# Two transformer layers with a routed mixture of experts: router weights folded with the modulation, and the last two tiles' residual sums and some of their norm statistics moved to TensorE and ScalarE

## The chip, the core and the metric

The kernel runs on one core of a Trainium2 chip. The metric is the device time of one execution, in microseconds. Beside the timed executions one more was profiled, and every row of a trace below is from that one.

## What is computed

Two layers. In each, 256 latent tokens (and in layer 0 also 256 context tokens) of width 1024 go through a token mixer, a residual sum with a layer norm, a modulated second layer norm, a router that picks 2 of 16 experts for a token, and the experts:

```python
p = modulate(h, mod[0], mod[1]) @ w_in + b_in
y = token_mix_out(p, ...)                       # ends in merged @ w_out + b_out
h = affine_ln(ALPHA * h + mod[2] * y, ln1_g, ln1_b)
m = hier_moe(modulate(h, mod[3], mod[4]), ...)  # modulate(x, shift, scale) = layer_norm(x) * (1 + scale) + shift
h = affine_ln(ALPHA * h + mod[5] * m, ln2_g, ln2_b)
...
glog, elog = tok @ rg_w + rg_b, tok @ re_w + re_b    # hier_moe: 4 groups, 16 experts
gsel = argmax(glog); top_v, top_i = top_k(elog of that group, 2)
out = sum over the chosen experts of weight * (silu(tok @ w_gate) * (tok @ w_up)) @ w_down
```

`mod` is six vectors of 1024 from one matrix product with the conditioning vector, a set for latent and a set for context tokens. Layer 1 needs latent tokens alone.

## The kernel before

Tokens are worked on in tiles of 128: in layer 0 tiles 2 and 3 are context and 0 and 1 latent, in layer 1 there are tiles 0 and 1. A tile keeps its tokens on the 128 partitions, its 1024 channels along the free axis.

Weights come in 512 KB pieces on SyncE's DMA queue, which issues in the order of the program and waits whenever the buffer of the next piece isn't free. Weights that need nearly full precision are split by ScalarE (`wh`) and VectorE (`wl`, or POOL) into two parts and multiplied in three matmuls of the fp32r type. Transposes (`tr`, L260) and other plain fp32 products (`mm`, L257) are TensorE matmuls; a plain fp32 matmul stands in the trace as two records.

The part of a layer around the change is `mix_out`. `merge` ends just before it; `mix_out` splits `merged` into `xh` and `xl`, then runs `wout` for the context tiles (layer 0 alone) and for the latent tiles, whose products ScalarE scales into `yT`, channels on partitions. `norms(tt)` transposes `yT` back in four 128 x 128 blocks for each half of a tile, VectorE adds `ALPHA * h` out of PSUM (L1206), `norm_affine` (L444 to L448) takes the first norm's statistics (`a0bst`, `a1bst`, `a0brs`, ...), and writes `h`; a second `norm_affine` with the modulation rows writes `xm` (statistics `b0...`, `b1...`), and POOL's queue sends `xm` to DRAM (`h2s`), from where the experts gather their tokens. `logits(tt)` (L1213 on) transposes `xm`, ScalarE copies it to `h2Tt`, and eight 20-column matmuls per tile with the router weights `rw` make `plog`. `route` (L1238) adds the bias `rb` into `lg` (L1242) and picks groups and experts; `rank` counts tokens of each expert and ends in `mxi` (L1311). Then every engine loads `mxi` and branches on it (L1603, L1604), and the experts start.

After the last `wout` there is no more weight work in layer 1 until the branch: what runs is this tail of norms, logits and route. In layer 0 the tail also has half of layer 1's modulation in it: `pump` hands out groups `psg<-w,silc` on TensorE over 16 pieces of `w_mod`, whose result (bank 2) goes to `mt`, `mods` in DRAM, and in part transposed into `modT` (L388 to L412). The order of the instructions on an engine is that of a scheduler at build time, so it interleaves the parts.

In layer 0 the latent tiles' `h` is loaded on POOL's queue and the position table added to it on POOL (L453 to L456) well before; POOL also does the `wl` splits of the latent `wout`.

## Time and profile before

| what | value |
|---|---|
| time of 3 runs | 1872.6, 1880.85, 1885.78 us (median 1880.85) |
| the profiled execution's own time | 1872.98 us |
| its span, first to last instruction | 1871.2 us |
| granted TensorE clock, mean | 0.958 of full speed |
| TensorE busy | 1716.1 us, 92% of the span |
| VectorE, ScalarE, POOL busy | 64%, 45%, 12% |
| DMA | 396.50 MB, 212 GB/s over the span |

The engines are PE (TensorE matmuls), PEld (its weight loads), DVE (VectorE), ACT (ScalarE), POOL (GpSimd) and SP (SyncE, DMA issue). Names as `psmm<-ident,yT` are the tile written and the tiles read, without buffer numbers. A line such as L257 can be that of a helper. A row of a timeline gives the start, the duration, the engine, the line, the operation, its operands and their shapes, how many instructions follow each other, and in square brackets how long the engine stood idle before and what ended that.

### The profile page before, as it was taken

What the parts mean: (1) busy time and instruction counts of PE and PEld (TensorE: products, weight loads), DVE (VectorE), ACT (ScalarE), POOL (GpSimd) and SP (SyncE); (2) the same over time, 40 slices, a digit from 0 to 9 for tenths busy, and PEclk for the clock granted to TensorE, in tenths of its full rate; (3) what the DMA queues carried; (4) which work ended last, traced back from release to release, by engine and by line L of the source; (5) the groups of instructions that cost most, each with busy time, mean ns of one, the idle gap of its engine ahead of it and who ended that gap; (6) DMA issues with size and microseconds to landing.
All of it is one profiled execution on the core that took longest, in us unless ns stands there. A gap on an engine that the chain in (4) does not pass through costs nothing. (4 is left out here: it accounts for less than half of the span.)

```text
span 1871.2 us, 31716 instructions
## 1 busy us (share of the span) xinstructions
PE 1716.1 (92%) x11399; PEld 1268.0 (68%) x11399; DVE 1204.7 (64%) x2623; ACT 851.3 (45%) x1696; POOL 223.1 (12%) x321
## 2 busy tenths in 40 slices
...
GB/s 342 90 75 46 13 24 152 197 84 130 169 130 192 300 144 188 304 295 398 392 382 376 345 314 77 66 92 58 47 147 149 169 327 168 324 414 406 403 410 136
DMA packets 112732, 396.50 MB, mean 212 GB/s; under 512 B 16256, under 2 KB 16352, under 8 KB 112560
## 3 DMA queue, kind: packets, MB, share of 16 engines
...
## 5 line engine op out<-in xcount | busy, mean ns | idle before, releaser
L266 ACT ACTIVATE wh<-w 128x512 fp32r<-128x512 f32 x500 | 310.1, 630 | 416.8 <-PE psmm L257 293.0
L263 DVE TENSOR_TENSOR wl<-w,wh 128x512 fp32r<-128x512 f32 x484 | 333.3, 700 | 188.6 <-ACT wh L266 185.2
L257 PE MATMUL psmm<-xh,wh 128*128 128x256 f32 (+1 forms) x1280 | 440.1, 344 | 1.3 <-ACT wh L266 1.3
L257 PE MATMUL psmm<-xh,wl 128*128 128x256 f32 (+1 forms) x1280 | 434.8, 340 | 4.0 <-POOL wl L263 2.9
L257 PE MATMUL psmm<-xl,wh 128*128 128x256 f32 (+1 forms) x1280 | 433.1, 339 | 2.0 <-DVE xl L263 2.0
L257 PEld LDWEIGHTS psmm<-xh,wh 128*128 128x128 f32 x1280 | 243.1, 190 | 52.5 <-issue 16.0
L257 PEld LDWEIGHTS psmm<-xh,wl 128*128 128x128 f32 x1280 | 243.0, 190 | 38.7 <-issue 5.9
L257 PEld LDWEIGHTS psmm<-xl,wh 128*128 128x128 f32 x1280 | 243.3, 190 | 30.0 <-issue 3.9
L970 DVE SCALAR_TENSOR_TENSOR cx<-cbuf,part,cx 128x512 f32<-128x512 f32 (+1 forms) x240 | 143.0, 614 | 2.1
L257 PE MATMUL psmm<-br,wh 128*128 128x512 f32 (+1 forms) x512 | 127.9, 337 | 0.4 <-ACT cth L266 0.4
L263 DVE TENSOR_TENSOR hid<-hid,psmm 128x256 f32<-128x256 f32 (+1 forms) x32 | 17.2, 537 | 136.6 <-PE psmm L257 121.6
L257 PEld LDWEIGHTS psmm<-br,wh 128*128 128x128 f32 x512 | 87.6, 188 | 11.7 <-ACT cth L266 0.6
L263 DVE TENSOR_TENSOR xh<-w,xh 128x512 fp32r<-128x512 f32 x124 | 80.5, 686 | 18.9 <-ACT xh L266 17.9
L257 PE MATMUL psmm<-br,wl 128*128 128x512 f32 (+1 forms) x256 | 86.4, 338 | 1.1 <-DVE wl L263 1.1
L257 PE MATMUL psmm<-xh,xTh 128*128 128x512 f32 x224 | 79.4, 413 | 5.7 <-ACT xh L266 5.1
L266 ACT ACTIVATE xh<-w 128x512 fp32r<-128x512 f32 x124 | 72.2, 627 | 18.9 <-DMA w<-in_expert_w_gate_dram 7.2
L257 PE MATMUL psg<-w,silc 128*32 128x512 f32 x320 | 64.2, 651 | 16.3 <-DMA w<-in_wmod_dram 16.3
L257 PE MATMUL psmm<-w,xTh 128*64 128x256 f32 x560 | 67.6, 387 | 1.6 <-DMA w<-in_expert_w_up_dram 1.1
L266 ACT ACTIVATE ye<-psmm,m 128x512 f32<-128x512 f32 x46 | 30.3, 684 | 71.5 <-PE psmm L257 71.1
L257 PEld LDWEIGHTS psmm<-w,xTh 128*64 128x64 f32 x560 | 41.0, 139 | 26.6 <-issue 5.1
L257 PEld LDWEIGHTS psmm<-xh,xTh 128*128 128x128 f32 x224 | 40.9, 189 | 24.5 <-ACT xh L266 9.7
L266 ACT ACTIVATE xTh<-psg 128x512 fp32r<-128x512 f32 (+1 forms) x46 | 26.3, 598 | 65.4 <-PE psg L260 62.0
...
## 6 DMA issues: line engine op xcount, KB each, us to landing
...
```

Of the source, the lines that this page charges most:

```text
L257: self.nc.tensor.matmul(out, lhsT, rhs, start=start, stop=stop, **k)
L263: (eng or self.nc.vector).tensor_tensor(out, a, b, op)
L266: self.nc.scalar.activation(out, in_, func, **k)
L970: nc.vector.scalar_tensor_tensor(x, w, dw[:, c, k:k + 1], x, op0=ALU.mult, op1=ALU.add)
```

## The change

1. `router_fold` (new): for each of latent and context tokens the router weights are multiplied by (1 + scale) of the modulation, each column's mean over the channels is taken off (a matmul with ones gives the column sums), and shift times the weights plus the bias goes into a constant `rwc`. A logit is then (weights of that kind times `h`), times the reciprocal deviation of the second norm, plus `rwc`: one small VectorE operation per tile writes `lg`. So `logits` transposes `h`, the first norm's result, and needs of the second norm the deviation `rs` alone; `modulate` still writes `xm` for `h2s`. `mod_rows` now transposes bank 2 of the modulation as well (four transposes, two copies more a layer) and leaves the 1 to be added at another place.
2. `norms_last` (new): for tiles 0 and 1, h + y / ALPHA is summed in PSUM by TensorE: for each half of a tile four fp32 matmuls of 128 columns (`yT` times identity) and one of 512 columns (identity times `h`). The first norm's epsilon is divided by ALPHA squared to match. Tile 0's first statistics are read by VectorE from PSUM. Tile 1's first statistics and both tiles' second ones are taken by ScalarE (`norm_sums`: a copy that also accumulates the sum, then a square with the mean as bias that accumulates the squares). Tiles 2 and 3 keep `norms`, with a plain addition at L1206's place.
3. The 256-column constant `pre` is dropped; its one user, inside the branch for more than 128 tokens of an expert, makes it anew.

```diff
@@ -396,17 +397,15 @@
                 nc.sync.dma_start(self.mods[l][:, o:o + 512], rows[64 * hf + 32 * m:64 * hf + 32 * m + 2, :])
-        if b == 2:
-            return
         pt = self.ps()
...
         for hf in hfs:
-            for m in ((0, 1), (0,))[b]:
+            for m in ((0, 1), (0, 1), (0,))[b]:
                 o = 64 * hf - p0 + 32 * m
                 dst, src = mt[:, 2 * b + m, 4 * hf:4 * hf + 4, :], v[:, :, o:o + 2]
-                if m:
+                if m and b == 0:
                     nc.vector.tensor_scalar(dst, src, 1.0, None, op0=ALU.add)
@@ -419,17 +418,34 @@
-    def norm_stats(self, src, tag):
+    def norm_stats(self, src, tag, eps=None):
         nc = self.nc
...
         rs = self.sb([P, 1], tag + "brs")
-        nc.vector.bn_stats(st[:, 0], src[:, 0:512])
-        nc.vector.bn_stats(st[:, 1], src[:, 512:1024])
+        a, b = src if isinstance(src, list) else (src[:, 0:512], src[:, 512:1024])
+        nc.vector.bn_stats(st[:, 0], a)
+        nc.vector.bn_stats(st[:, 1], b)
         nc.vector.bn_aggr(ag, st)
-        self.act(rs, ag[:, 1:2], AF.Sqrt, bias=self.eps, scale=1.0)
+        self.act(rs, ag[:, 1:2], AF.Sqrt, bias=self.eps if eps is None else eps, scale=1.0)
         nc.vector.reciprocal(rs, rs)
         return ag[:, 0:1], rs
+    def norm_sums(self, src, u, eps, copy, junk):
+        rs, st, nm = (self.sb([P, w], f"{n}{u}") for w, n in ((1, "lrs"), (4, "lst"), (2, "lnm")))
+        if isinstance(src, list):
+            for q in range(2):
+                self.act(copy[:, 512 * q:512 * q + 512], src[q], AF.Identity, accum_out=st[:, q:q + 1])
+            self.act(nm[:, 0:1], st[:, 0:1], AF.Identity, scale=-1.0 / D)
+            self.act(nm[:, 1:2], st[:, 1:2], AF.Identity, scale=-1.0 / D, bias=nm[:, 0:1])
+            src = copy
+        else:
+            self.act(junk, src, AF.Identity, accum_out=st[:, 0:1])
+            self.act(nm[:, 1:2], st[:, 0:1], AF.Identity, scale=-1.0 / D)
+        self.act(junk, src, AF.Square, bias=nm[:, 1:2], accum_out=st[:, 2:3])
+        self.act(rs, st[:, 2:3], AF.Sqrt, bias=eps, scale=1.0 / D)
+        self.nc.vector.reciprocal(rs, rs)
+        return nm[:, 1:2], rs
@@ -1158,6 +1174,25 @@
+    def router_fold(self, l, s):
+        nc = self.nc
+        rw = self.rw.rearrange("p (k n) -> p k n", k=KD)
+        shift, scale = self.modT[l][:, 3, :, s], self.modT[l][:, 4, :, s]
+        w = self.sb([P, KD, 20], "rwf") if s else rw
+        c = self.sb([P, 20], f"rwc{s}")
+        t = self.sb([P, 256], "xm")
+        part = t[:, 160:200].rearrange("p (i n) -> p i n", i=2)
+        tv = t[:, 0:160].rearrange("p (k n) -> p k n", k=KD)
+        self.tt(tv, rw, shift[:, :, None].to_broadcast([P, KD, 20]))
+        nc.vector.tensor_reduce(part[:, 0], tv.rearrange("p k n -> p n k"), AX.X, ALU.add)
+        self.tt(w, rw, scale[:, :, None].to_broadcast([P, KD, 20]))
+        nc.vector.tensor_reduce(part[:, 1], w.rearrange("p k n -> p n k"), AX.X, ALU.add)
+        pt = self.ps()
+        self.mm(pt[:, 0:40], self.ones, t[:, 160:200], True, True)
+        self.tt(c, pt[:, 0:20], self.rb, ALU.add)
+        nc.vector.scalar_tensor_tensor(w, pt[:, None, 20:40].to_broadcast([P, KD, 20]), -1.0 / D, w, op0=ALU.mult, op1=ALU.add)
+        return w, c
     def mix_out(self, l, ntt):
@@ -1176,8 +1211,8 @@
         m2 = self.modT[l][:, 2]
-        nc.vector.tensor_scalar(s1, m2, 0.5, None, op0=ALU.mult)
-        self.tt(s2, m2, self.pp("b_out")[:, :, None].to_broadcast([P, KD, 2]))
+        nc.vector.tensor_scalar(s1, m2, 0.5 / ALPHA, None, op0=ALU.mult)
+        nc.vector.scalar_tensor_tensor(s2, m2, 1.0 / ALPHA, self.pp("b_out")[:, :, None].to_broadcast([P, KD, 2]), op0=ALU.mult, op1=ALU.mult)
         g1, b1 = self.row(l, "big", 0, 0), self.row(l, "big", 1, 0)
@@ -1193,8 +1228,10 @@
-        rw = self.rw.rearrange("p (k n) -> p k n", k=KD)
+        fold = self.fold
         plog = self.ps("g")
+        self.lg = self.sb([P, 4, 20], "lg")
         def norms(tt):
@@ -1203,43 +1240,74 @@
                 c = slice(512 * q, 512 * q + 512)
-                nc.vector.scalar_tensor_tensor(x[:, c], h1[:, c], ALPHA, pt, op0=ALU.mult, op1=ALU.add)
-            self.norm_affine(h1, x, g1, b1, f"a{tt % 2}")
+                self.tt(x[:, c], h1[:, c], pt, ALU.add)
+            mu, rs = self.norm_stats(x, f"a{tt % 2}", self.epsa)
+            nc.vector.scalar_tensor_tensor(x, x, mu, g1, op0=ALU.subtract, op1=ALU.mult)
+            nc.vector.scalar_tensor_tensor(h1, x, rs, b1, op0=ALU.mult, op1=ALU.add)
+            mu, rs = self.norm_stats(h1, f"b{tt % 2}")
+            return x, mu, rs, ALU.subtract
+        def norms_last():
+            pts = []
+            for tt in (0, 1):
+                pts.append([self.ps("g" if tt == 0 else "mm") for _ in range(2)])
+                for q, pt in enumerate(pts[tt]):
+                    for k in range(4):
+                        self.mm(pt[:, 128 * k:128 * k + 128], yT[:, 4 * q + k, 128 * tt:128 * tt + 128], self.ident, k == 0, False, skip_group_check=True)
+                    self.mm(pt, self.ident, self.h[:, tt, 512 * q:512 * q + 512], False, True, skip_group_check=True)
+            x0, x1 = self.sb([P, D], "xm"), self.sb([P, D], "xm")
+            mu, rs = self.norm_stats(pts[0], "a0", self.epsa)
+            nm1, rs1 = self.norm_sums(pts[1], 0, self.epsa, x1, self.h[:, 1])
+            for q in range(2):
+                c = slice(512 * q, 512 * q + 512)
+                nc.vector.scalar_tensor_tensor(x0[:, c], pts[0][q], mu, g1[:, c], op0=ALU.subtract, op1=ALU.mult)
+            nc.vector.scalar_tensor_tensor(self.h[:, 0], x0, rs, b1, op0=ALU.mult, op1=ALU.add)
+            nc.vector.scalar_tensor_tensor(x1, x1, nm1, g1, op0=ALU.add, op1=ALU.mult)
+            nc.vector.scalar_tensor_tensor(self.h[:, 1], x1, rs1, b1, op0=ALU.mult, op1=ALU.add)
+            return [(x, *self.norm_sums(self.h[:, tt], tt, self.eps, None, x), ALU.add) for tt, x in enumerate((x0, x1))]
+        def modulate(tt, x, mu, rs, op):
             m3, m4 = ms[tt // 2]
-            self.norm_affine(x, h1, m4, m3, f"b{tt % 2}", x)
+            nc.vector.scalar_tensor_tensor(x, self.h[:, tt], mu, m4, op0=op, op1=ALU.mult)
+            nc.vector.scalar_tensor_tensor(x, x, rs, m3, op0=ALU.mult, op1=ALU.add)
             nc.gpsimd.dma_start(self.h2s[128 * tt:128 * tt + 128, :], x)
-            return x
-
-        def logits(tt, x):
+        def logits(tt, rs):
+            rw, c = fold[tt // 2]
             hT = self.sb([P, KD, P], "h2Tt")
...
                 for k in range(4):
-                    self.tr(pt[:, 128 * k:128 * k + 128], x[:, 512 * q + 128 * k:512 * q + 128 * k + 128])
+                    self.tr(pt[:, 128 * k:128 * k + 128], self.h[:, tt, 512 * q + 128 * k:512 * q + 128 * k + 128])
                 self.act(hT[:, 4 * q:4 * q + 4, :].rearrange("p k t -> p (k t)"), pt)
...
                 self.mm(plog[:, 20 * tt:20 * tt + 20], hT[:, k, :], rw[:, k, :], k == 0, k == KD - 1)
+            nc.vector.scalar_tensor_tensor(self.lg[:, tt], plog[:, 20 * tt:20 * tt + 20], rs, c, op0=ALU.mult, op1=ALU.add)
...
         xs = {}
-        for s in reversed(range(ns)):
-            wout(s)
-            for tt in (2 * s, 2 * s + 1):
+        if ns == 2:
+            wout(1)
+            for tt in (2, 3):
                 xs[tt] = norms(tt)
+                modulate(tt, *xs[tt])
+        wout(0)
+        xs[0], xs[1] = norms_last()
         for tt in range(2, ntt):
-            logits(tt, xs[tt])
+            logits(tt, xs[tt][2])
         self.pump(1)
-        logits(0, xs[0])
-        logits(1, xs[1])
+        for tt in (0, 1):
+            modulate(tt, *xs[tt])
+        for tt in (0, 1):
+            logits(tt, xs[tt][2])
         self.pump(3)
-        self.plog = plog
+        self.h2t = [xs[0][0], xs[1][0]]
         self.dump(f"h1_{l}", self.h[:, :ntt])
...
         v = nc.vector
-        lg = self.sb([P, 4, 20], "lg")
-        v.tensor_tensor(lg[:, :T], self.plog[:, :20 * T].rearrange("p (t n) -> p t n", t=T), self.rb[:, None, :].to_broadcast([P, T, 20]), ALU.add)
+        lg = self.lg
         gl = lg[:, :T, 0:4]
@@ -1750,6 +1819,7 @@
             self.merge(l, 1, br, nt, False)
+            self.fold = {s: self.router_fold(l, s) for s in reversed(range(nt // 256))}
             self.mix_out(l, ntt)
```

How the instructions stand at three places; `psmm`, `psg` are PSUM tiles, numbers are buffers.

Layer 1's tail on TensorE, behind the last `wout` matmul, before:

```order
L260 MATMUL psmm_17591<-ident_77,yT_17300 128x128 x4
L260 MATMUL psmm_17597<-ident_77,yT_17300 128x128 x4
L260 MATMUL psmm_17625<-ident_77,yT_17300 128x128 x4
L260 MATMUL psmm_17631<-ident_77,yT_17300 128x128 x4
L260 MATMUL psmm_17659<-ident_77,xm_17590 128x128 x4
L260 MATMUL psmm_17665<-ident_77,xm_17590 128x128 x4
L257 MATMUL psg_17301<-rw_9194,h2Tt_17658 128x20 x8
L260 MATMUL psmm_17680<-ident_77,xm_17624 128x128 x4
L260 MATMUL psmm_17686<-ident_77,xm_17624 128x128 x4
L257 MATMUL psg_17301<-rw_9194,h2Tt_17679 128x20 x8
```

and now, from the second half of tile 0 on (the first half has the same two rows ahead of it):

```order
L256 MATMUL psg_17650<-ident_79,yT_17358 128x128 x4
L256 MATMUL psg_17650<-h_17325,ident_79 128x512
L256 MATMUL psmm_17661<-ident_79,yT_17358 128x128 x4
L256 MATMUL psmm_17661<-h_17325,ident_79 128x512
L256 MATMUL psmm_17662<-ident_79,yT_17358 128x128 x4
L256 MATMUL psmm_17662<-h_17325,ident_79 128x512
L259 MATMUL psmm_17721<-ident_79,h_17325 128x128 x4
L259 MATMUL psmm_17727<-ident_79,h_17325 128x128 x4
L256 MATMUL psg_17359<-rw_9240,h2Tt_17720 128x20 x8
L259 MATMUL psmm_17743<-ident_79,h_17325 128x128 x4
L259 MATMUL psmm_17749<-ident_79,h_17325 128x128 x4
L256 MATMUL psg_17359<-rw_9240,h2Tt_17742 128x20 x8
```

The 16 transposes of `yT` became sums with `h`, and the transposes ahead of the logits read `h` and no longer `xm`. On ScalarE in the same tail, from the table load on, before:

```order
L266 ACTIVATE a0brs_17605<-a0bag_17604,eps_69 128x1
L266 ACTIVATE a1brs_17639<-a1bag_17638,eps_69 128x1
L266 ACTIVATE b0brs_17615<-b0bag_17614,eps_69 128x1
L266 ACTIVATE h2Tt_17658<-psmm_17659 128x512
L266 ACTIVATE h2Tt_17658<-psmm_17665 128x512
L266 ACTIVATE b1brs_17649<-b1bag_17648,eps_69 128x1
L266 ACTIVATE h2Tt_17679<-psmm_17680 128x512
L266 ACTIVATE h2Tt_17679<-psmm_17686 128x512
```

and now, from the first copy of a transposed `h` on (the six rows ahead of these are tile 0's deviation and tile 1's first norm, with the accumulators `lst` and the means `lnm`):

```order
L265 ACTIVATE h2Tt_17720<-psmm_17721 128x512
L265 ACTIVATE xm_17673,lst_3330_17699<-h_17325 128x1024
L265 ACTIVATE h2Tt_17720<-psmm_17727 128x512
L265 ACTIVATE lnm_3331_17700<-lst_3330_17699 128x1
L265 ACTIVATE xm_17673,lst_3330_17699<-h_17325,lnm_3331_17700 128x1024
L265 ACTIVATE xm_17674,lst_3333_17707<-h_17325 128x1024
L265 ACTIVATE lrs_3329_17698<-lst_3330_17699,eps_69 128x1
L265 ACTIVATE lnm_3334_17708<-lst_3333_17707 128x1
L265 ACTIVATE h2Tt_17742<-psmm_17743 128x512
L265 ACTIVATE xm_17674,lst_3333_17707<-h_17325,lnm_3334_17708 128x1024
L265 ACTIVATE h2Tt_17742<-psmm_17749 128x512
L265 ACTIVATE lrs_3332_17706<-lst_3333_17707,eps_69 128x1
```

The copies into `h2Tt` stand between full-width passes over `h`.

Layer 0, VectorE where `merge` ends and `wout` begins, before:

```order
L263 TENSOR_TENSOR wl_6195<-w_6192,wh_6194 128x512
L263 TENSOR_TENSOR xl_6121<-merged_2504,xh_6120 128x512 x3
L1149 SCALAR_TENSOR_TENSOR mt_6104<-cth_6089,psmm_6091 128x512
L263 TENSOR_TENSOR xl_6121<-merged_2504,xh_6120 128x512
L263 TENSOR_TENSOR merged_2504<-merged_2504,mt_6104 128x512
L263 TENSOR_TENSOR xl_6121<-merged_2504,xh_6120 128x512 x4
```

and now (`rwf` and `rw` are the weights of context and latent tokens, the two `rwc` their constants):

```order
L262 TENSOR_TENSOR xm_6130<-rw_239,modT_29_140 128x160
L1187 TENSOR_REDUCE xm_6130<-xm_6130 128x20
L262 TENSOR_TENSOR rw_239<-rw_239,modT_29_140 128x160
L262 TENSOR_TENSOR xl_6153<-merged_2506,xh_6152 128x512
L1189 TENSOR_REDUCE xm_6130<-rw_239 128x20
L262 TENSOR_TENSOR xl_6153<-merged_2506,xh_6152 128x512
L1165 SCALAR_TENSOR_TENSOR mt_6115<-cth_6100,psmm_6102 128x512
L262 TENSOR_TENSOR rwc_1194_6119<-psmm_6125,rb_240 128x20
L262 TENSOR_TENSOR merged_2506<-merged_2506,mt_6115 128x512
L1193 SCALAR_TENSOR_TENSOR rwf_6118<-psmm_6125,rwf_6118 128x160
L262 TENSOR_TENSOR rwc_1197_6129<-psmm_6135,rb_240 128x20
L1193 SCALAR_TENSOR_TENSOR rw_239<-psmm_6135,rw_239 128x160
```

Eight small operations came between the splits `xl` that TensorE's `wout` waits for.

Layer 0's tail on TensorE, up to the last groups of the modulation, before:

```order
L257 MATMUL psg_6155<-rw_237,h2Tt_6932 128x20 x8
L257 MATMUL psg_6923<-w_7109,silc_66 32x512 x2
L257 MATMUL psg_6923<-w_7111,silc_66 32x512 x2
L257 MATMUL psg_6923<-w_7117,silc_66 32x512 x2
L260 MATMUL psmm_6954<-ident_77,xm_6834 128x128 x4
L260 MATMUL psmm_6960<-ident_77,xm_6834 128x128 x4
L257 MATMUL psg_6923<-w_7119,silc_66 32x512 x2
L257 MATMUL psg_6155<-rw_237,h2Tt_6953 128x20 x8
L257 MATMUL psg_6923<-w_7125,silc_66 32x512 x2
L257 MATMUL psg_6923<-w_7127,silc_66 32x512 x2
L257 MATMUL psg_6923<-w_7133,silc_66 32x512 x2
```

and now, the last such groups, which stand behind the counting matmuls of `rank`:

```order
L256 MATMUL psg_6955<-w_7163,silc_66 32x512 x2
L256 MATMUL psg_6955<-w_7165,silc_66 32x512 x2
L256 MATMUL psg_6955<-w_7171,silc_66 32x512 x2
L256 MATMUL psg_6955<-w_7173,silc_66 32x512 x2
L259 MATMUL psmm_7186<-ident_79,mt_6952 128x128 x4
L1672 TENSOR_LOAD mxi_7139
```

Four more groups and four transposes of `mt` now stand directly ahead of the branch's load of `mxi`.

## Rows read from the trace of the kernel before

**Rows 1.** The page, part 1: busy time, share of the span, instructions of each engine.

```profile
PE 1716.1 (92%) x11399; PEld 1268.0 (68%) x11399; DVE 1204.7 (64%) x2623; ACT 851.3 (45%) x1696; POOL 223.1 (12%) x321
```

**Rows 2.** Table by stretch, layer 1's tail and the experts after it.

```profile
core 0: us, PE busy (x) PEld busy (x) DVE busy (x) ACT busy (x) POOL busy (x), PEclk, DMA share, GB/s
1560.00:1565.00 5.00, 0.00 (x0) 0.00 (x0) 5.00 (x9) 0.29 (x1) 0.00 (x0) 0.86 1.01 406
...
1570.00:1575.00 5.00, 4.98 (x23) 4.77 (x24) 4.86 (x7) 1.49 (x3) 0.54 (x1) 0.50 0.26 105
...
1580.00:1585.00 5.00, 0.86 (x5) 0.75 (x4) 3.41 (x21) 0.00 (x0) 0.00 (x0) 0.50 0.00 0
...
1650.00:1800.00 150.00, 144.10 (x878) 88.03 (x878) 59.92 (x124) 58.80 (x109) 23.53 (x24) 1.00 1.02 407
```

**Rows 3.** Timeline of TensorE, layer 1's tail.

```profile
1556.65 2.02 PE L260 MATMUL psmm<-ident,yT 128*128 128x128 f32 x16
1570.02 1.94 PE L260 MATMUL psmm<-ident,xm 128*128 128x128 f32 x8 [11.34 <-DVE xm L448]
1571.79 3.60 PE L257 MATMUL psg<-rw,h2Tt 128*128 128x20 f32 x16
```

**Rows 4.** Timeline of VectorE, layer 1's tail.

```profile
1557.29 1.28 DVE L1206 SCALAR_TENSOR_TENSOR xm<-h,psmm 128x512 f32<-128x512 f32 x2 [4.64 <-PE psmm L260]
1558.49 0.69 DVE L427 BATCH_NORM_STATS2 a0bst<-xm 128x6 f32<-128x512 f32 x1
...
1569.79 1.28 DVE L448 SCALAR_TENSOR_TENSOR h<-xm,a1brs,rowt 128x1024 f32<-128x1024 f32 x1
...
1574.06 1.29 DVE L448 SCALAR_TENSOR_TENSOR xm<-xm,b1brs,rowt 128x1024 f32<-128x1024 f32 x1
1580.90 0.20 DVE L1242 TENSOR_TENSOR lg<-psg,rb 128x40 f32<-128x40 f32 x1 [5.56 <-PE psg L257]
```

**Rows 5.** Timeline of VectorE, layer 0's tail.

```profile
776.20 0.24 DVE L1242 TENSOR_TENSOR lg<-psg,rb 128x80 f32<-128x80 f32 x1 [7.19 <-PE psg L257]
...
788.26 0.42 DVE L395 TENSOR_SCALAR mt<-mt 32x512 f32<-32x512 f32 x1
```

**Rows 6.** Timeline of TensorE, layer 0's tail.

```profile
747.17 2.26 PE L260 MATMUL psmm<-ident,yT 128*128 128x128 f32 x16
...
761.55 1.05 PE L257 MATMUL psg<-w,silc 128*32 128x512 f32 x4 [1.92 <-DMA w<-in_wmod_dram]
...
774.20 1.96 PE L257 MATMUL psg<-rw,h2Tt 128*128 128x20 f32 x16
```

**Rows 7.** Timeline of TensorE in layer 0: two plain fp32 products of other stages.

```profile
387.06 1.02 PE L257 MATMUL psmm<-wsT,ones 128*128 128x512 f32 x2
...
404.88 1.06 PE L257 MATMUL psmm<-wsT,vln 128*128 128x128 f32 x8
```

**Rows 8.** Timeline of ScalarE, layer 1's tail.

```profile
1560.51 0.29 ACT L266 ACTIVATE a0brs<-a0bag,eps 128x1 f32<-128x1 f32 x1 [1.79 <-DVE a0bag L429]
...
1571.14 0.60 ACT L266 ACTIVATE h2Tt<-psmm 128x512 f32<-128x512 f32 x1 [4.65 <-PE psmm L260]
```

**Rows 9.** Groups by line and form, ScalarE: count, then busy us, mean ns.

```profile
L266 ACT ACTIVATE w<-h,m0nm,m0brs 128x1024 f32<-128x1024 f32 x2 | 2.5, 1242 | 0.9 <-DVE m0nm L441 0.9
```

**Rows 10.** Timeline of SyncE's DMA queue, layer 0's tail: start, time over which issued.

```profile
757.94 14.69 SPq L375 DMA_DIRECT2D w<-in_wmod_dram  x11
774.31 0.33 SPq L1538 DMA_DIRECT2D w<-in_expert_w_gate_dram  x1
```

**Rows 11.** Timeline of VectorE, layer 0, the same place.

```profile
693.62 1.90 DVE L263 TENSOR_TENSOR xl<-merged,xh 128x512 fp32r<-128x512 f32 x3 [0.41 <-ACT xh L266]
...
697.23 2.49 DVE L263 TENSOR_TENSOR xl<-merged,xh 128x512 fp32r<-128x512 f32 x4
```

**Rows 12.** Timeline of TensorE, layer 0, the end of `merge`.

```profile
691.88 0.62 PE L257 MATMUL psmm<-br,wh 128*128 128x512 f32 x2
```

**Rows 13.** Timeline of POOL, layer 0, `h` plus positions, and the later splits.

```profile
650.64 2.40 POOL L263 TENSOR_TENSOR h<-h,xm 128x1024 f32<-128x1024 f32 x1 [7.77 <-DMA xm<-in_pos_dram]
...
714.44 5.35 POOL L263 TENSOR_TENSOR wl<-w,wh 128x512 fp32r<-128x512 f32 x4 [24.79 <-ACT wh L266]
```

10 lines of the change are left out of this document (6 added, 4 removed).

## The prediction

> **What bounds the kernel now.** The page's first part comes first: TensorE is busy 92% of the span [rows 1], so time can be won only where it has nothing to do. The table by stretch shows such a place behind layer 1's last `wout`: TensorE busy 0.00 of 5 us from 1560 on, VectorE 5.00 of 5 [rows 2]. The timelines name the chain there: after the 16 transposes of `yT` at 1556.65 TensorE stands idle 11.34 us until `xm` is there [rows 3]; VectorE works without a gap from 1557.29 to the last `xm` at 1574.06 + 1.29 = 1575.35 and then waits 5.56 us for the logits, so `lg` starts at 1580.90 [rows 4]. From the end of `wout` to `lg` that is 24.25 us, all of it path. What is won there should reach the end one for one: DMA moves nothing from 1580 to 1585, because no buffer is free, and is full (share 1.02) from 1650 to 1800, so the expert weights' stream starts earlier by as much [rows 2].
>
> Layer 0's tail is the same chain with other work beside it. `lg` starts at 776.20 and VectorE's last operation ahead of the branch ends at 788.26 + 0.42 = 788.68 [rows 5]. TensorE has modulation groups to run, and these wait for DMA (1.92 us at 761.55) [rows 6].
>
> **Layer 1's tail, the gain.** The change puts more on TensorE and takes work from VectorE. One half of a tile costs four 128-column products (1.06 us for eight records, that is four products; in a dense row I take 0.21 each) and one of 512 columns (1.02 for its two records, the last one's tail in it; I take 0.87) [rows 7]: 4 x 0.21 + 0.87 = 1.7 us, 6.8 for four halves against 2.02 for the transposes [rows 3]. The halves are then ready at 1558.4, 1560.1, 1561.8 and 1563.5.
>
> VectorE's two half-width additions per tile and six of eight statistics passes (0.69 each [rows 4]) leave its chain. ScalarE gets, for tile 1, two accumulating half-width copies from PSUM (0.60, the price of an `h2Tt` copy [rows 8]), two means (0.29 each [rows 8]), one full-width square (1.24 [rows 9]) and the root (0.29). From 1563.5: 0.60 + 0.29 gives 1564.4, the square 1565.7, the root 1566.0. VectorE's product of `x1` must wait for the square, which reads `x1`: 1565.7 + 1.28 + 1.28 puts `h` of tile 1 at about 1568.5, where it was 1569.79 + 1.28 = 1571.07 [rows 4].
>
> From there ScalarE is the chain. From 1566.0 it still does three full-width passes and four copies, then one more pass: 4 x 1.24 + 4 x 0.60 + 4 x 0.29 = 8.5 us, and I add 0.3 for hand-overs between engines, so that the last root ends at 1574.8 and the last square, 0.60 + 0.29 ahead of it, at 1573.9. VectorE's `modulate` of tile 1 stands ahead of the last `lg` and waits for that square and that root: 1573.9 + 1.28 + 1.28 = 1576.5, with the reciprocal between. The last logits are no later: half of a tile's 16 records, 3.60 / 2 = 1.8 us [rows 3], behind the last copy at 1574.5. So the last `lg` ends at about 1576.8; before it was 1580.90 + 0.20 = 1581.10 [rows 4]. **Gain 4.3 us.** The trace has no accumulating activation. From below it costs no more than the plain one; from above, an extra 0.29 on each of eight (a small activation of its own [rows 8]), of which some five lie on the chain and half are hidden by `modulate`'s fixed end: I take nothing extra, and keep 3.0 to 4.5.
>
> The Trainium skill speaks against this part ("ScalarE: Activation LUTs", Rules for kernel authors: for additions and products use VectorE, not ScalarE). That is rival B. The rows bear the rule out in price alone: two full-width passes cost 2 x 1.24 on ScalarE [rows 9], two half-width ones 2 x 0.69 on VectorE [rows 4].
>
> The granted clock is at 0.86 from 1560, after TensorE has been idle, and at 0.50 from 1570 [rows 2], the lower level of 1.2 GHz: a logit record takes 3.60 / 16 = 0.225 us there and 1.96 / 16 = 0.12 in layer 0 [rows 3, 6]. TensorE now works on until 1563.5 and rests some 5 us instead of 11.34 before the transposes of tile 0. I count no higher clock; if it stayed up, the last eight logits would cost 0.9 us less, but `modulate` sets the end.
>
> **Layer 0's tail, the gain.** The way to the start of the last `lg` takes 1576.6 - 1556.65 = 19.95 us in layer 1, from 747.17 on that is 767.1; some fourteen records of modulation groups at 1.05 / 4 stand between the transposes and the logits [rows 6], 3.7 us, so it starts at 770.8 and ends at about 771.05, where it was 776.20 + 0.24 = 776.44 [rows 5]: 5.4 us. But the modulation's groups must now end ahead of the branch on TensorE, and the last four stand behind `rank` together with the transposes of `mt`. Their 16 pieces go through buffers that groups free: eleven were issued from 757.94 to 772.63, the expert's gate weights behind them at 774.31 [rows 10]. TensorE's first groups are later now by the longer sums (4.7 us), so I let the last piece land at 779.8, its groups take 1.05 [rows 6], and VectorE's `mt` pieces, two copies and a split (0.69 + 2 x 0.42 + 4 x 0.2 + 0.69, 3.0 us) end at 783.8. The old way from `lg` to the last operation, 788.68 - 776.44 = 12.24 us, would end at 783.3 by itself, so the two ends lie close. 788.68 - 783.8: **gain 4.9 us**; 0 if the stream's end moves to 785 and what follows it stays, 5.4 if it hides.
>
> **The fold, the cost.** In layer 0 eight small operations came ahead of six of the eight splits `xl` on VectorE, which TensorE's `wout` waits for. Four are 160 wide, two reduce 160 to 20, two are 20 wide. Nearest from below is `lg`, 0.24 [rows 5], from above a 512-wide pass, 1.90 / 3 = 0.63 [rows 11]: 1.9 to 5.0 us. The shapes lie nearer the small one; 4 x 0.30 + 2 x 0.40 + 2 x 0.22 = 2.4. The first also waits for a buffer of `merge`'s operand `br`, read until after 691.88 [rows 12], and two are held until TensorE has summed the columns (a product behind `merge` and a way back, 0.2 to 0.6). The splits stood at 693.62 and 697.23 and are needed one by one, so nearly all of it is path: **2.5 us, 1 to 3.5**. In layer 1 one fold is all, four of its operations run long before, and two small ones and the matmul stay: 0.5 (0.2 to 1). Bank 2's eight transposes cost 8 x 0.13 [rows 6], a half of them on the path: 0.5.
>
> **No cost taken.** POOL now adds the positions after `merge`, in the tile that `br` frees: one addition waited 7.77 us for its load after others before it, so I give the loads 12 us from 692, and two additions at 2.40 end at about 709, ahead of the splits at 714.44 [rows 13]; if late, the latent `wout` waits 4 to 5 us. `modulate` and `h2s` end later against `lg`, but the gather needs the whole selection first. Tiles 2 and 3 keep their price, and the constant's bytes are nothing.
>
> **Sum.** -4.3 - 4.9 + 2.5 + 0.5 + 0.5 = -5.7 us against the profiled execution's 1872.98, hence 1867.3. That execution is 7.9 us under the median of 1880.85, and a median of the changed kernel is to be expected where before's is: 1880.85 - 5.7 = 1875.
>
> **Rivals.**
> - A, slower. Layer 0's stream decides: pieces are freed late as TensorE is held by sums and logits, the last four groups, `mt`'s transposes and its copies come ahead of the branch on both engines. For: 1.92 us of DMA wait at 761.55 already [rows 6]. Against: the stream has ten us until `lg`. It turns where the last piece lands after 785. Layer 0 then gains nothing or loses 1, the fold takes 3.5, the two small costs 1.0, layer 1 gives 3.0: +1.5 to +2.5, or 1883.
> - B, ScalarE's chain is dearer. Each accumulation costs 0.3 and each dependent step a further hand-over. For: five more full-width passes in one order with the copies. Against: ScalarE stood idle 4.65 us before `h2Tt` [rows 8]. Both gains halve: -4.6 + 3.5 = -1.1, or 1880.
> - C, POOL's additions are late: 4.5 us given back, -5.7 + 4.5 = -1.2, or 1879.6.
> - D, it goes better: the fold hides under `merge` and layer 0's wait for the weights shrinks: the gains stay at 9.2, some 1 us comes on top and the costs go: -10, or 1871.
> - E, the change does not shorten what it says, because `modulate` or the order holds `lg` back as before: 0 + 3.5, or 1884.
>
> Chances: forecast 0.48, A 0.15, B 0.17, C 0.06, D 0.10, E 0.04. All are within 1% of 1880.85 (18.8 us, about what a measurement of this kernel can tell). The three runs span 13.3 us, so a median of such runs can lie 5 us to either side of its kernel. Range 1864 to 1886: forecast, B, C and D, and half of A. Faster by over 1% 0.06, within 1% 0.90, slower 0.04: both ends only by something outside these cases.
>
> **What would show it.** In the changed profile: four rows of sums at 1.7 us each on TensorE behind both last `wout`s; ScalarE without a gap of over 1 us from tile 1's copies to the last `h2Tt`; the last `lg` ended some 20.2 us after layer 1's `wout` (24.45 before); in layer 0 the last `mt` copy 36.6 us after `wout` (41.5 before); small VectorE rows of 0.2 to 0.4 before the `xl` splits, TensorE waiting 2 to 3 us there. The forecast is wrong if the sums take over 2.2 us each, if an accumulating pass takes over 1.5, or if layer 0's branch is no earlier than before.

## The result, and the profile after

The changed kernel is slower: 1892.01 us median of 13 runs against 1879.75 of 13 of the kernel before, a ratio of 1.0069 (1.0047 to 1.009), some 13 us, where 5.7 us less were forecast and 1864 to 1886 given as the range. Its profiled execution has a span of 1885.9 us, 14.7 over that of before; TensorE is busier by 15 us and still 92% of the span ([rows 1] before):

```profile
PE 1731.3 (92%) x11461; PEld 1272.5 (67%) x11461; DVE 1201.1 (64%) x2630; ACT 866.0 (46%) x1732; POOL 224.2 (12%) x321
```

**Layer 1's tail did what was forecast.** TensorE's timeline shows the sums in the place of the transposes of [rows 3]: eight records of 128 columns, then the 512-column product, 1.75 us for each half. ("Behind `wout`" means, here and below, from the first TensorE record behind the last `wout` matmul: 1576.60 in this tail and 760.59 in layer 0's, 1556.65 and 747.17 before.)

```profile
1576.60 1.05 PE L256 MATMUL psg<-ident,yT 128*128 128x128 f32 x8
1577.49 1.02 PE L256 MATMUL psg<-h,ident 128*128 128x512 f32 x2
...
1586.95 3.42 PE L256 MATMUL psg<-rw,h2Tt 128*128 128x20 f32 x16 [1.74 <-ACT h2Tt L265]
...
1592.83 3.58 PE L256 MATMUL psg<-rw,h2Tt 128*128 128x20 f32 x16 [0.67 <-DVE lg L1285]
```

ScalarE takes a full-width accumulating pass in 1.15 us and reads the accumulator in 0.19 more, where 1.24 had been taken for both ([rows 9]); the small root is as in [rows 8]:

```profile
1584.85 1.15 ACT L265 ACTIVATE h<-xm,lnm 128x1024 f32<-128x1024 f32 x1
1585.90 0.19 ACT L265 ACTIVATION_READ_ACCUMULATOR h<-xm,lnm 128x1 f32 x1
1586.12 0.29 ACT L265 ACTIVATE lrs<-lst,epsa 128x1 f32<-128x1 f32 x1
```

On VectorE the last `lg` ends at 1596.68, 20.08 us behind `wout` (forecast 20.2, before 24.45, [rows 3, 4]). It waited 0.67 us for the last logits, the 16 records at 1592.83, which had waited 0.67 us for `lg` of tile 0. The first operation behind the branch waits 5.07 us:

```profile
1596.44 0.24 DVE L1285 SCALAR_TENSOR_TENSOR lg<-psg,lrs,rwc 128x20 f32<-128x20 f32 x1 [0.67 <-PE psg L256]
...
1610.60 0.29 DVE L1395 TENSOR_TENSOR oe<-ohg,oh 128x32 f32<-128x32 f32 x2 [5.07 <-DVEq L1673]
```

**Layer 0, between `merge` and `wout`, lost 7.2 us.** VectorE's timeline ([rows 11] before): the fold's eight operations take 0.16 to 0.45 each, 2.5 together, but the six splits `xl` behind them take 8.03 us, where six took some 3.7.

```profile
698.84 0.32 DVE L262 TENSOR_TENSOR xm<-rw,modT 128x160 f32<-128x160 f32 x1
699.20 0.45 DVE L1187 TENSOR_REDUCE xm<-xm 128x20 f32<-128x160 f32 x1
...
703.20 8.03 DVE L262 TENSOR_TENSOR xl<-merged,xh 128x512 fp32r<-128x512 f32 x6
```

Four of the six take 0.68 as before. The second and the third take 2.85 each:

```profile
703.80 2.85 DVE L262 TENSOR_TENSOR xl<-merged,xh 128x512 fp32r<-128x512 f32 x1
```

```profile
706.57 2.85 DVE L262 TENSOR_TENSOR xl<-merged,xh 128x512 fp32r<-128x512 f32 x1
```

TensorE waits for the splits, 0.79, 1.91 and 1.36 us; the last two waits end as these two splits do:

```profile
703.94 0.38 PE L256 MATMUL psmm<-xl,wh 128*128 128x256 f32 x1 [0.79 <-DVE xl L262]
...
706.70 0.55 PE L256 MATMUL psmm<-xl,wh 128*128 128x256 f32 x1 [1.91 <-DVE xl L262]
...
709.48 0.58 PE L256 MATMUL psmm<-xl,wh 128*128 128x256 f32 x1 [1.36 <-DVE xl L262]
```

POOL's two additions of the positions, which were over by 653 before ([rows 13]), run just there. Each takes about as long as the split that began beside it, and each of the two splits ends 0.55 us behind an addition (706.65 behind 706.10, 709.42 behind 708.87):

```profile
703.33 2.77 POOL L262 TENSOR_TENSOR h<-h,xm 128x1024 f32<-128x1024 f32 x1 [2.67 <-DMA xm<-in_pos_dram]
```

```profile
706.06 2.81 POOL L262 TENSOR_TENSOR h<-h,xm 128x1024 f32<-128x1024 f32 x1
```

**Layer 0's tail got longer by 5 us.** SyncE's queue ([rows 10] before): two pieces of `w_mod` leave at 774.94, the other nine from 781.49 to 795.57, that is 14 and from 21 to 35 us behind `wout`, where the eleven left 10.8 to 25.5 us behind it.

```profile
774.94 0.80 SPq L376 DMA_DIRECT2D w<-in_wmod_dram  x2
...
781.49 14.08 SPq L376 DMA_DIRECT2D w<-in_wmod_dram  x9
795.66 0.39 SPq L1607 DMA_DIRECT2D w<-in_expert_w_gate_dram  x1
```

TensorE had pieces in the chip. Ten records on them run between 771.89 and 777.8, but the 18 in a row, which ran 9.7 us behind `wout` before (756.87), run at 780.41, 19.8 us behind it: behind the sums, the transposes of all four tiles and the logits of three. The last group waits 1.72 us for its piece until 800.72, and the transposes of `mt` follow ([rows 6] before):

```profile
760.59 1.05 PE L256 MATMUL psg<-ident,yT 128*128 128x128 f32 x8
...
780.41 2.76 PE L256 MATMUL psg<-w,silc 128*32 128x512 f32 x18
...
800.72 1.05 PE L256 MATMUL psg<-w,silc 128*32 128x512 f32 x4 [1.72 <-DMA w<-in_wmod_dram]
803.55 1.08 PE L259 MATMUL psmm<-ident,mt 128*128 128x128 f32 x4 [1.78 <-DVE mt L396]
```

VectorE's last `lg` is there early, 24.8 us behind `wout` (29.3 before). The counts then wait 4.59 us, because TensorE's groups stand ahead of `selb` and wait for DMA; yet they end in `mxi` at 799.3, ahead of the last group, so this wait does not set the end. `mt`, `modT` and a split come last, to 805.51, 44.9 us behind `wout` (41.5 before), and the first operation behind the branch starts 5.5 us later, at 810.99 (3.9 later before, at 792.59, [rows 5]): 50.4 us behind `wout` where it was 45.4. Why 1.6 us more pass at the branch itself is not shown.

```profile
785.11 0.24 DVE L1285 SCALAR_TENSOR_TENSOR lg<-psg,lrs,rwc 128x20 f32<-128x20 f32 x1 [0.58 <-PE psg L256]
...
794.27 0.23 DVE L1351 SCALAR_TENSOR_TENSOR posp<-psmm,selb 128x64 f32<-128x64 f32 x1 [4.59 <-PE psmm L256]
...
801.82 0.69 DVE L262 TENSOR_TENSOR mt<-psg,mt 128x512 f32<-128x512 f32 x1 [2.49 <-PE psg L256]
...
804.67 0.24 DVE L411 COPY modT<-psmm 128x8 f32<-128x8 f32 x2 [0.55 <-PE psmm L259]
...
810.99 0.36 DVE L1395 TENSOR_TENSOR oe<-ohg,oh 128x64 f32<-128x64 f32 x2 [5.48 <-DMA rowt<-in_rows_dram]
```

### The profile page after: what moved, and what is told of

It reads as the page before. It is cut to its first block, busy times and chain, and to the rows that moved or that the text cites. A ratio compares the mean times of both kernels' runs of the same rounds, so it can differ in the third digit from the quotient of the medians.

```text
span 1885.9 us, 31891 instructions
## 1 busy us (share of the span) xinstructions
PE 1731.3 (92%) x11461; PEld 1272.5 (67%) x11461; DVE 1201.1 (64%) x2630; ACT 866.0 (46%) x1732; POOL 224.2 (12%) x321
## 5 line engine op out<-in xcount | busy, mean ns | idle before, releaser
L256 PEld LDWEIGHTS psmm<-w,xTh 128*64 128x64 f32 x560 | 41.2, 140 | 27.0 <-issue 6.0
```

Source lines behind the costliest of these rows:

```text
L256: self.nc.tensor.matmul(out, lhsT, rhs, start=start, stop=stop, **k)
```

## The experiments

All were timed against the kernel before, 6 to 12 runs each. A kernel's time moves by 8 to 22 us between executions, so the table is the sharper view. It gives, from each profile, the time from one row to another in the kernel before and what each kernel adds: between ScalarE's 1st, 12th, 24th and 36th gate `cth` in layer 0's `merge`, from there to the first and to the last `yT` of `wout`, on to the group maximum `gmx` and to VectorE's first operation behind the branch (`oe`); for layer 1 from the first to the last gate, from the last `yT` to `gmx`, and to `oe`. Between gates 1 and 12 and gates 24 and 36 TensorE's granted clock was 1.00 in every trace, so there tenths of a us tell. Between gates 12 and 24 it was 0.974 to 0.992 (0.983 before), in layer 1's gates 0.956 to 0.994 (0.994 before), and in late_positions it was 0.958 in `wout` (1.00 in the others): a us or two in these columns can be the clock's.

| kernel | gates 1-12 | 12-24 | 24-36 | to wout | wout | to maximum | to branch | L1 gates | L1 to maximum | L1 to branch |
|---|---|---|---|---|---|---|---|---|---|---|
| before, us | 151.73 | 199.02 | 105.80 | 8.34 | 47.11 | 28.63 | 16.12 | 290.62 | 24.28 | 13.41 |
| changed | +1.18 | +2.87 | +1.15 | +7.17 | +0.53 | -4.51 | +9.49 | +0.53 | -4.37 | +0.48 |
| after_again | +1.15 | +2.31 | +1.14 | +7.17 | +0.55 | -4.51 | +10.84 | +0.86 | -4.38 | +0.56 |
| own_scratch | +1.15 | +2.33 | +1.14 | +0.68 | +0.58 | -4.51 | +11.89 | +0.42 | -4.37 | +0.57 |
| late_positions | +0.00 | -0.69 | +0.00 | +4.57 | +2.49 | -0.41 | +0.10 | +2.80 | -0.00 | -0.05 |
| pump_first | +1.15 | +0.78 | +1.15 | +6.99 | -0.40 | -3.11 | +4.26 | +2.09 | -4.36 | +0.52 |
| before_moved | +1.15 | +0.96 | +1.14 | -0.00 | -0.07 | +0.41 | -0.31 | +0.55 | -0.01 | -0.01 |
| moved_back | +0.00 | +1.30 | -0.01 | +0.68 | -0.02 | +1.00 | +3.18 | +1.24 | -0.07 | +0.51 |
| moved_back_pump | +0.00 | +1.21 | +0.00 | +0.67 | +0.67 | +1.89 | +3.18 | +0.07 | +0.30 | +0.18 |
| moved_back_l1 | +0.02 | +0.08 | +0.00 | +0.68 | +0.63 | -2.15 | +5.89 | +1.02 | -0.07 | +0.02 |
| mended | -0.01 | +1.31 | +0.00 | +0.67 | +0.63 | -4.51 | +9.62 | +1.11 | -4.36 | +0.27 |
| late_columns | -0.02 | +1.38 | +0.00 | +0.68 | +0.64 | -4.51 | +7.68 | +14.47 | -4.37 | +0.05 |
| late_columns_pump | +0.01 | +1.62 | +0.00 | +0.67 | +0.67 | -3.22 | +3.42 | +12.77 | -4.37 | +0.02 |
| late_columns_l1 | -0.01 | +1.40 | +0.00 | +0.68 | +0.60 | -4.44 | +0.04 | +16.26 | -4.37 | +0.06 |
| columns_in_sgu_l1 | -0.02 | +1.32 | +0.00 | +0.68 | +0.64 | -4.38 | -0.02 | -0.12 | -4.36 | +0.05 |
| columns_in_sgu_pump | -0.02 | +1.39 | -0.01 | +0.67 | +0.67 | -0.53 | +1.35 | +1.10 | -4.36 | +0.52 |
| tiles_up_32 | +1.22 | +0.18 | +1.30 | +0.00 | +0.98 | +0.01 | -0.19 | +3.89 | -0.00 | -0.02 |
| tiles_up_64 | +0.97 | -0.09 | +1.07 | +0.00 | +0.74 | +0.29 | -0.28 | +1.94 | -0.00 | +0.11 |

**The changed kernel again.**

> The changed kernel once more, to see what of the trace repeats. Theory: the 7.2 us that the place between merge and wout of layer 0 lost, the 4 to 5 us that layer 0's tail lost and the 4.2 us that layer 1's tail won are the change's and repeat within 0.5 us; the 5.4 us by which everything ahead of that place was late (same instructions in both kernels) are not, and lie between 0 and 6 in another execution. Rival: these 5.4 us repeat too, so the change slows the projections and the merge ahead of it. Ratio to the kernel before 1.005 to 1.009 in both.

1.0074 (1.0046 to 1.0102). Fold, both tails and `merge` repeat within 0.6 us, but for the way to the branch (9.5 and 10.8). So in `merge` 1.15 + 1.15 us are the change's, and a part of the 2.3 to 2.9 between gates 12 and 24: the rival holds there. What lies ahead of `merge` moves by chance: the first gate starts at 236.36 in one execution of the changed kernel and at 241.23 in the other.

**Scratch in a ring of its own.**

```diff
-        t = self.sb([P, 256], "xm")
+        t = self.sb([P, 256], "hid")
```

> The changed kernel, with the fold's scratch tiles in the ring of `hid`, which lies unused until the experts, in place of the ring that the position tiles need. So POOL adds the positions early again, as before the change, and the fold's sums are taken long before. Theory 1 (POOL's two additions ran beside VectorE's six splits `xl` and doubled their time, 8.03 us for six, and TensorE's wout waited 4.1 us for them): the six splits take 3.6 to 4 us, TensorE's waits there fall below 1 us, the kernel is 5 to 6 us faster than the changed one, ratio to before 1.003 to 1.005. Rival (the fold's eight small operations are the cost): 1 to 2 us faster, splits still slow, ratio 1.006.

The splits are at their old price, VectorE's row:

```profile
708.23 3.09 DVE L262 TENSOR_TENSOR xl<-merged,xh 128x512 fp32r<-128x512 f32 x5
```

and the place costs 0.68 in place of 7.17 us: theory 1 is right there, and the fold costs 0.7 when the half of it that needs no `merge` runs early. Yet the ratio is 1.0075 (1.0048 to 1.0102), not 1.003 to 1.005 as expected: layer 0's way to the branch took 11.9, 1 to 2.4 us more than in the changed kernel, so some was given back where the stream ends late, and 5 us lie within the two intervals.

**Late positions alone, in the kernel before.**

```diff
+            for _ in range(nt // 256):
+                t = self.sb([P, 256], "xm")
+                nc.vector.memset(t[:, 160:200], 0.0)
+                self.mm(self.ps()[:, 0:40], self.ones, t[:, 160:200], True, True)
             self.mix_out(l, ntt)
```

> The kernel before, with nothing of the change but two idle scratch tiles (set to zero, read by a product with ones whose result nobody uses) that take the position tiles' buffers until merge ends, so POOL adds the positions beside the splits xl as in the changed kernel. Theory 1: some six of the splits take 1.2 to 1.35 us each in place of 0.6, wout of layer 0 starts late by 3.5 to 4.5 us, ratio to before 1.002. Rival: the splits keep 0.6 us and nothing is lost, 0 to +0.5 us.

4.57 us lost at the place, with nothing of the fold: four splits take 6.83 us on VectorE while POOL adds. Again two of them make up the loss, with 2.86 and 2.83 us, and the other two take 0.68; it is not the 1.2 to 1.35 for each of six that was expected.

```profile
699.96 6.83 DVE L263 TENSOR_TENSOR xl<-merged,xh 128x512 fp32r<-128x512 f32 x4
```

```profile
700.03 5.60 POOL L263 TENSOR_TENSOR h<-h,xm 128x1024 f32<-128x1024 f32 x2 [2.37 <-DMA xm<-in_pos_dram]
```

Ratio 1.0014 (0.9991 to 1.0037). That the late additions delay `wout` is shown by the trace; by time they can't be told from nothing. What is left of the 7.17 us of the changed kernel, 2.6, is about what the fold's eight late operations take (2.5).

**The modulation's groups first** (own edit on the changed kernel; pieces already in the chip run ahead of the sums).

```diff
         wout(0)
+        self.pump(2)
         xs[0], xs[1] = norms_last()
```

> The changed kernel, with two of the steps of layer 1's modulation (eight groups of TensorE, on pieces that are in the chip already) handed out ahead of the last two tiles' sums in place of behind them. Theory 2 (layer 0's tail got longer because the pieces of w_mod were freed 10 us later, TensorE doing sums, transposes and logits first, so that the stream's last piece landed late and branch and experts waited for it): the next piece is issued within 4 us of the last wout matmul, not 14 to 21 us behind it, the operation of VectorE that comes last ahead of the branch ends 38 to 40 us after the last wout matmul (44.9 in the changed kernel, 41.5 before), and the kernel is 4 to 7 us faster than the changed one, ratio to before 1.003 to 1.005. Rival (the number of instructions ahead of the branch decides, four transposes and copies of mt): 0 to 1 us.

The next pieces leave 1.6 us behind `wout`, `lg` is 1.4 us later, and the way from the last `yT` to `oe` is 3.8 us shorter than in the changed kernel, 1.15 us longer than before it. The last group ends 33.3 us behind `wout`, where it ended at 41.2 (35.5 before), so the stream no longer sets the end; VectorE's last operation, which ends 42.6 us behind `wout`, not 38 to 40 as expected, now comes behind the counts of `rank` and the transposes of `mt`. Ratio 1.0063 (1.0036 to 1.0089): theory 2 by the trace, not to be told from nothing by time.

**The addresses.** The kernel before, with `pre` dropped and the new small tiles allocated:

```diff
-         ("half", 2), ("lvl", 128), ("pre", 256), ("first4", 4), ("key0", 16), ("hoff", 1))
+         ("half", 2), ("lvl", 128), ("first4", 4), ("key0", 16), ("hoff", 1))
...
+            for n, m in (("rwf", 160), ("rwc1", 20), ("rwc0", 20), ("lrs0", 1), ("lrs1", 1)):
+                if l == 0:
+                    nc.vector.memset(self.sb([P, m], n)[:, 0:1], 0.0)
```

> The kernel before with its tiles at the addresses of the changed kernel and nothing else of the change: the constant `pre` dropped (made anew inside the branch that isn't taken) and the small tiles that the change adds allocated but not used. In the four executions seen so far of kernels made from the changed one, layer 0's merge (from the first to the last gate activation, 456.55 us in the kernel before, the same instructions) took 3.1 to 5.2 us longer, and in a kernel made from the one before 0.7 us less; dense 512-column matmuls follow each other 1% slower. Theory 3 (it is the addresses: `w`, `wh`, `wl` lie 992 bytes and `xh`, `xl`, `merged` 96 bytes lower): the stretch takes 459.5 to 462 us, ratio to before 1.002 to 1.003. Rival (it is not the addresses, but chance or something else in the program): 455.5 to 457 us, ratio 0.999 to 1.001.

Gates 1 to 12 and 24 to 36 take 1.15 and 1.14 longer, as in the changed kernel. Rows of the 1st and 12th gate in the kernel before (151.73 us apart):

```profile
235.84 0.67 ACT L266 ACTIVATE cth<-psmm,hbg 128x512 f32<-128x512 f32 x1
...
387.57 0.67 ACT L266 ACTIVATE cth<-psmm,hbg 128x512 f32<-128x512 f32 x1
```

in the changed kernel (152.91):

```profile
236.36 0.67 ACT L265 ACTIVATE cth<-psmm,hbg 128x512 f32<-128x512 f32 x1
...
389.27 0.67 ACT L265 ACTIVATE cth<-psmm,hbg 128x512 f32<-128x512 f32 x1
```

and in this one, which has the instructions of before (152.88):

```profile
241.14 0.67 ACT L265 ACTIVATE cth<-psmm,hbg 128x512 f32<-128x512 f32 x1
...
394.02 0.67 ACT L265 ACTIVATE cth<-psmm,hbg 128x512 f32<-128x512 f32 x1
```

The sum over `merge` is 3.25 us, the middle part at the granted clock of before (0.983); the time, 1.0002 (0.9979 to 1.0025), doesn't show it. The other way round, the changed kernel with `pre` back and its new tiles inside old ones:

```diff
-        rs, st, nm = (self.sb([P, w], f"{n}{u}") for w, n in ((1, "lrs"), (4, "lst"), (2, "lnm")))
+        st, nm = (self.sb([P, w], f"{n}{u}") for w, n in ((4, "lst"), (2, "lnm")))
+        rs = st[:, 3:4]
...
-        w = self.sb([P, KD, 20], "rwf") if s else rw
-        c = self.sb([P, 20], f"rwc{s}")
-        t = self.sb([P, 256], "xm")
+        t = self.sb([P, 512], "hid")
+        w = t[:, 256:416].rearrange("p (k n) -> p k n", k=KD) if s else rw
+        c = t[:, 416:436]
```

> The changed kernel with its new tiles in the ring of `hid`, so that all other tiles up to the experts' lie where they lay before the change; the positions are thereby early again too (as in own_scratch). Theory 3: layer 0's merge takes 455.5 to 457.5 us, against 459.6 to 461.8 in the kernels at the changed addresses, and the kernel is 3 to 5 us faster than own_scratch, ratio to before 1.004 to 1.006. Rival: merge stays at 459.6 or more, ratio 1.007.

0.00 and -0.01: the addresses slow `merge`. Of the 1.3 us that stay between gates 12 and 24, the transposes of layer 0's bank 2 take 0.6: from gate 21 to gate 23 it is 19.91 us in place of 19.28. The rest can't be told from the granted clock (0.974, before 0.983). The transposes, with their wait, in the trace of the kernel named mended below:

```profile
568.82 0.66 PE L260 MATMUL psmm<-ident,mt 128*128 128x128 f32 x4 [0.54 <-DVE mt L395]
```

Ratio 1.0054 (1.0033 to 1.0075); both tails had lost their gain, by my edit: the deviation shared a tile with the accumulators, so tile 0's second statistics waited for tile 1's `h`. The same fault is in two kernels run with it, moved_back_pump (1.0057) and moved_back_l1 (1.003). In the latter the sums are in layer 1 alone, so its layer 0 has neither sums nor that fault; yet its tail there is 3.7 us longer than before (-2.15 + 5.89), taken up again below. Mended:

```diff
-        st, nm = (self.sb([P, w], f"{n}{u}") for w, n in ((4, "lst"), (2, "lnm")))
-        rs = st[:, 3:4]
+        if u:
+            st = self.sb([P, 8], "lst1")
+            nm, rs = st[:, 4:6], st[:, 6:7]
+        else:
+            rs, st, nm = (self.sb([P, w], f"{n}{u}") for w, n in ((1, "lrs"), (4, "lst"), (2, "lnm")))
```

> moved_back without its own fault: there the reciprocal deviation and the accumulators shared one tile, so that tile 0's second statistics waited for tile 1's result (both tails lost their gain, layer 1's last lg came 24.2 us after wout's last scaling, as before the change); here the deviation has a tile of its own again. So this is the changed kernel with all tiles at the old addresses and the positions early. Theory (addresses 3 to 5 us, positions 6.5 us are the whole of what the changed kernel lost outside of layer 0's tail): layer 1's gain is back, 4.4 us, merge of layer 0 takes 456 to 457.5 us, wout of layer 0 starts within 0.7 us of the place it had before, layer 0's tail still loses 4 to 7 us; ratio to before 1.001 to 1.003. Rival (something else slows the changed kernel too): 1.004 or more.

Rows of the gates again (151.72):

```profile
241.38 0.67 ACT L266 ACTIVATE cth<-psmm,hbg 128x512 f32<-128x512 f32 x1
...
393.10 0.67 ACT L266 ACTIVATE cth<-psmm,hbg 128x512 f32<-128x512 f32 x1
```

1.0033 (1.0013 to 1.0053): layer 1's gain is back, and what is lost is in layer 0's tail, 5.1 us (-4.51 + 9.62).

**Which tile.** The kernel before with `xh`, `xl`, `merged` and the tiles of the layer's own pools higher, `w`, `wh`, `wl` and `br` where they were, by one or two idle tiles of 32 bytes:

```diff
+            for n in range(1):
+                if l == 0:
+                    nc.vector.memset(self.sb([P, 1], f"pad{n}")[:, 0:1], 0.0)
             self.mix_out(l, ntt)
```

> The kernel before with `xh`, `xl`, `merged` and all tiles of the layer's own pools 32 bytes higher, `w`, `wh`, `wl`, `br` unmoved. The moving operand `xh`, `xl` then begins at 105728, a multiple of 64 as in the changed kernel (105600), where it began at 105696, 32 above a multiple of 64. Theory 3a (the multiple of 64 of the moving operand decides): dense 512-column matmuls follow each other 1% slower, layer 0's merge takes 459 to 462 us (456.55 before; its part between the first and the twelfth gate 1.15 us longer). Rival 3b (the address of `wh`, `wl` or `br` decides, or larger blocks): 455.5 to 457 us.

> The same with 64 bytes: `xh` begins at 105760, 32 above a multiple of 64 as before the change. Theory 3a: layer 0's merge as in the kernel before, 455.5 to 457 us, ratio to before 1.000. Rival (any move of `xh` against `wh` costs): 459 us or more.

+1.22 and +1.30 by 32 bytes, +0.97 and +1.07 by 64; `wout` slows down as well (+0.98, +0.74). Layer 1's gates took longer too, but at a lower granted clock (0.983 and 0.988, before 0.994). Ratios 1.0028 (1.0005 to 1.0051) and 1.0031 (1.0006 to 1.0055). Theory 3a falls: it isn't a multiple of 64. That it costs to move these tiles against `w`, `wh`, `wl` is shown, by which rule stays open.

**Bank 2's columns after the branch** (the mended kernel; loaded from `mods` in layer 1, ahead of the last `merge`).

```diff
+        if l == 1 and b == 2:
+            return
+        self.mod_cols(b, hfs, rows, mt)
...
+            if l == 1:
+                rows = self.sb([P, 512], "hid")
...
+                    nc.gpsimd.dma_start(rows[64 * hf:64 * hf + 2, :], self.mods[1][:, 4 * D + 512 * hf:4 * D + 512 * hf + 512])
+                self.mod_cols(2, range(2), rows, self.modT[1])
             self.merge(l, 1, br, nt, False)
```

> mended, with bank 2 of layer 1's modulation transposed not ahead of layer 0's branch but in layer 1 ahead of the last merge, from the copy of the rows in DRAM. It tells how much of layer 0's loss is the four transposes and two copies that stand last ahead of the branch (TensorE waits for VectorE's mt, VectorE for TensorE, about 2.5 us) and how much the late stream of w_mod. Theory 2 (mostly the stream): layer 0's tail gets 2 to 3 us shorter and stays 2 to 4 us longer than before the change; ratio to before 1.000 to 1.002. Rival (the transposes are all of it): 5 us or more shorter, tail at or below the 44.75 us of the kernel before, ratio 0.998.

Layer 0's way to the branch falls by 1.9 us to 7.68, but 1.7 of them lie ahead of the transposes: the last group ends 39.3 us behind `wout` in place of 41.0, though the last piece was issued at the same place. So this pair can't price the transposes. pump_first and late_columns_pump, with and without them, lie 0.95 us apart in layer 0's tail (+1.15 and +0.20). moved_back_l1 and late_columns_l1, without sums in layer 0, lie 8.1 us apart (+3.74 and -4.40); but in the trace of the former the granted clock was 0.57 from 762 to 769, close to the lower level of 1.2 GHz, after TensorE had been busy 5.00 of 5 us, and tile 0's logits took 2.93 us in place of 1.96. So what the transposes cost ahead of the branch stays open, and that the stream is the larger part, as theory 2 has it, rests on pump_first.

TensorE waited 9.69 us for the load in layer 1 (+14.47, ratio 1.009 (1.0064 to 1.0117)), and 9.7 and 10.6 us in late_columns_pump (1.0037) and late_columns_l1 (1.0065), the two kernels below with the load at that place.

**All faults out.** The load on SyncE's queue, ahead of the merge of branch 3 and in four partitions; the sums in layer 1's tail alone (`ns` is 2 in layer 0, 1 in layer 1):

```diff
+            if l == 1:
+                rows = self.sb([4, 512], "mt")
+                for hf in range(2):
+                    nc.sync.dma_start(rows[2 * hf:2 * hf + 2, :], self.mods[1][:, 4 * D + 512 * hf:4 * D + 512 * hf + 512])
             self.merge(l, 3, self.sgu(l, nt), nt, False)
...
+                for hf in range(2):
+                    nc.vector.tensor_copy(self.modT[1][:, 4, 4 * hf:4 * hf + 4, :], v[:, :, 2 * hf:2 * hf + 2])
...
         wout(0)
-        xs[0], xs[1] = norms_last()
+        if ns == 2:
+            xs[0], xs[1] = norms(0), norms(1)
+        else:
+            xs[0], xs[1] = norms_last()
```

> late_columns_l1 without its own fault: there the copy of the rows was loaded into `hid` on POOL's queue just ahead of the last merge, and TensorE waited 9.7 us for it (merge of layer 1 15 us longer). Here it is loaded on SyncE's queue ahead of the merge before the last but one and transposed from four partitions. Tiles at the old addresses, positions early, fold, sums and ScalarE's statistics in layer 1 alone. Theory (what the change can give without its three faults: addresses, late positions, layer 0's tail): merge of layer 1 within 1.5 us of the kernel before, layer 0's tail 40 to 41 us (44.75 before), layer 1's last lg 4.4 us earlier, fold and its transposes give back 3 to 4 us: 4 to 6 us faster than before, ratio 0.997 to 0.998. Rival: the place of the columns costs again, or layer 0's gain is lost to the DMA stream of the experts: ratio 1.000 or more.

1875.84 us against 1879.41, ratio 0.9976 (0.9955 to 0.9997): the one kernel whose interval lies below before's, some 16 us under the changed one. The pieces of `w_mod` leave 7.7 us behind its `wout` (10.8 before), the branch is taken 16.1 us behind the maximum as before, the maximum comes 4.38 earlier. So layer 0's tail gains 4.4 us with the folded logits, which need of the second norm only the deviation, and no sums on TensorE.

```profile
762.92 19.14 SPq L375 DMA_DIRECT2D w<-in_wmod_dram  x11
782.15 0.41 SPq L1622 DMA_DIRECT2D w<-in_expert_w_gate_dram  x1
```

```profile
779.89 0.24 DVE L1298 SCALAR_TENSOR_TENSOR lg<-psg,b1brs,hid 128x20 f32<-128x20 f32 x1 [0.98 <-PE psg L257]
...
792.81 1.29 DVE L263 TENSOR_TENSOR xh<-w,xh 128x512 fp32r<-128x512 f32 x2
...
796.26 0.36 DVE L1411 TENSOR_TENSOR oe<-ohg,oh 128x64 f32<-128x64 f32 x2 [2.16 <-DVEq L1688]
```

With the sums in both layers and `pump(2)` ahead of layer 0's:

> The same, but with the sums and ScalarE's statistics in both layers and two of the modulation's steps ahead of layer 0's sums (late_columns_pump without the fault). Theory 2: layer 0's tail as before the change (44.5 to 45.5 us), so 4 to 5 us slower than columns_in_sgu_l1, ratio to before 0.999 to 1.001: layer 0's tail has no room for the sums on TensorE. Rival (sums in layer 0 cost nothing once the stream is served): within 1 us of columns_in_sgu_l1.

Layer 0's tail takes 0.82 us more than before (-0.53 + 1.35), the other 4.40 less (-4.38 - 0.02): by the trace the sums, with ScalarE's statistics and the two steps of `pump`, cost layer 0's tail 5.2 us, as theory 2 has it. By time the two can't be told apart: 0.9981 (0.9958 to 1.0004).

## Why the prediction was wrong, point by point

By the table the changed kernel's trace is 14.5 us longer: +5.2 in layer 0's `merge`, +7.2 between `merge` and `wout`, +5.0 in layer 0's tail, -3.9 in layer 1's, and +1.1 elsewhere.

- **Layer 1's gain, 4.3 us: right**, 4.37 to the maximum, as VectorE's chain of passes was the path and ScalarE took part of it over. The last wait was another than forecast: `modulate` of tile 1 ended 19.2 us behind `wout` (19.85 forecast), and the last logits, 3.58 us at a granted clock of 0.50, ended 0.6 later. That the sum comes within 0.1 us is luck in part. Rival B did not come true: an accumulating pass costs 0.1 us more than taken (1.15 + 0.19), not 0.3. The rule of the Trainium skill ("ScalarE: Activation LUTs", Rules for kernel authors: VectorE, not ScalarE, for additions and products) holds here in price alone: two such passes take 2.7 us on ScalarE and two half-width ones 1.4 on VectorE ([rows 4]), and the move still pays, as VectorE had no gap.
- **Layer 0's gain, 4.9 us: wrong in sign, +5.** The step that failed is "I let the last piece land at 779.8", which is 32.6 us behind `wout`: it was used at 800.72, 40.1 behind. The forecast put off TensorE's groups by the 4.7 us of the longer sums; the 18 records came 10.1 us later, because the transposes of tiles 0 and 1 and the logits of tile 0 stood ahead of them too. VectorE's last operation then ended 44.9 us behind `wout`, where 36.6 was forecast. This is rival A (chance 0.15), whose condition, a last piece behind 785 or 37.8 us behind `wout`, came true at a higher price than its -1. pump_first, where these groups run ahead of the sums, shows the stream: 3.8 of the 5 us. What the transposes of `mt` add ahead of the branch stays open.
- **The fold, 2.5 us: right in size** for the kernel as it stands: its eight operations take 2.5 us on VectorE, and 2.6 us are left of the 7.2 when late_positions' 4.6 are taken off. That the two add up is an argument; no run has the late half of the fold alone.
- **"No cost taken" for the positions: wrong, 4.6 us alone, and 6.5 with the fold's late half (7.17 - 0.68).** The additions ended 10.8 us behind the last gate, earlier than forecast (16.6, 709 in the trace before), and ahead of the next splits on POOL. What failed is the cover: the forecast asked who waits for POOL, not what runs beside it. The trace before had the price: VectorE's full-width pass took 2.13 us at 740.73, where the same pass takes 1.29 in layer 1 with POOL idle ([rows 4]), while POOL split:

```profile
740.73 2.13 DVE L448 SCALAR_TENSOR_TENSOR xm<-xm,b1brs,rowt 128x1024 f32<-128x1024 f32 x1
```

```profile
739.65 4.35 POOL L263 TENSOR_TENSOR wl<-w,wh 128x512 fp32r<-128x512 f32 x2
```

- **"The constant's bytes are nothing": wrong, by the addresses.** Some 3.3 us in `merge` (before_moved), none of it in the forecast; no row of before could show it. Bank 2's transposes were put at 0.5 and cost 0.6 in layer 0's `merge` alone.
- **The range** held all rivals one at a time and no two of them together, nor a cost without a row.
